# Convolution taps and index scores read from PSUM, group B's gate tiles projected for all tokens at once, and a new order of steps

## The chip, the core and the metric

The kernel runs on one core of one Trainium2 chip. The metric is the device time of one execution in microseconds (us), as the median of several runs. A profile of one execution gives what each engine did and when: TensorE (PE, with its weight loads as PEld), VectorE (DVE), ScalarE (ACT), GpSimd (POOL) and SyncE (SP), which issues the loads.

## What is computed

One layer: an adaptive norm of x (1024 tokens, 1024 channels), one input projection into 3792 columns, two groups of heads, one output projection.

```python
h = rmsnorm(x, g_pre[layer]) * (1.0 + scale[:, None, :]) + shift[:, None, :]
proj = h @ w_in[layer]
(qkv_a, z_a, b_a, a_a, q_b, ckv, z_b, iq, ik, iw) = jnp.split(proj, list(SPLIT_OFFSETS), axis=-1)
o_a = gated_deltanet(qkv_a, z_a, b_a, a_a, ...)     # group A
o_b = dsa_sparse_attention(q_b, ckv, iq, ik, iw, ..., z_b)   # group B
mix = jnp.concatenate([o_a, o_b], axis=-1) @ w_out[layer]

def causal_conv(u, w):          # 4 taps, on q, k and v of group A
    up = jnp.pad(u, ((0, 0), (CONV_W - 1, 0), (0, 0)))
    out = up[:, 0:L] * w[0]
    for j in range(1, CONV_W):
        out = out + up[:, j:j + L] * w[j]
    return out

# the index scores of group B, whose 256 largest choose a query's keys (8 heads of 64)
rel = jnp.einsum('bqhd,bsd->bqhs', iqb, ik)
score = jnp.einsum('bqh,bqhs->bqs', iwb, jax.nn.relu(rel))
```

Group A is a gated DeltaNet over chunks of tokens. Group B attends over the chosen keys, and its output is multiplied by silu(z_b), the gate.

## The kernel before, in words

Channels lie on the partitions and tokens along the rows. A projection (`proj`, L427) takes 128 columns of the weights and one half of the tokens (512) and lays 24 matmuls into one PSUM bank: for each of eight slices of the input a high by high, a high by low and a low by high part of the numbers (L435 to L437), where weights and input are split in two parts that are exact for TensorE. The weights come from memory as `wraw`, and are split into `whi` (a copy, L177 or L179) and `wlo` (a difference, L184).

PSUM has eight banks, under three tags: "pp" with two (projections), "r" with four (scores, recurrence, attention) and "g" with two (transposes and small things). A matmul that begins a new product in a bank waits until the last reader of the product before it in that bank is done.

The program is cut into parts, and each part into steps. The list `PLAN` is an order of steps written by hand: K, Q, V (the projections and convolutions of keys, queries and values for a pair of heads 0 or 1), J (inverses on POOL), M (their merging on PE), R (the recurrence), N and A (norm and gate of group A), I (index queries and scores), S0 and S1 (the searches of each query's 256th largest score, S0 with its sums on ACT for the three longest blocks, S1 with counts on DVE), HQ (queries of group B), HZ (its gates), C (latent keys and values), T (attention), O (output). A step yields to those before it in the list, and a scheduler lays the instructions of the engines out from it. The table `ENGINES` names the engine for single sites ("V" DVE, "A" ACT, "G" POOL). What is on one engine runs in the order laid out, so a row that waits holds up those behind it.

`conv_half` (L730) takes a product of a tile of channels and half of the tokens. It copies the product to a tile `u` in SBUF (that has three columns ahead, for the taps that reach back), writes `cv` = last tap times product, and adds the other three taps from `u`: on DVE one instruction each (`add_scaled`, L193), or on ACT a multiplication into `tmp` (L198) and an addition on POOL (L201). SiLU follows in place (L742). `to_nat` (L789) then turns values by 128 columns, and evicts them as `vn`.

The score of a block of queries is summed head by head: two matmuls (the key's two parts, L585 and L586) into a bank of tag "r", the ReLU into a tile `relu` in SBUF (L589 on ACT, L591 on DVE), and `score += iw * relu` on DVE (L193), or on ACT and POOL. The queries' two parts, `qe` and `qo`, are finished on DVE (L570, L571).

`gate_b` is laid out twice, for the later half of the tokens (HZ0) and for the earlier (HZ1). Each takes the same four tiles of weights, so these are loaded and split twice.

Of the kernel before, what the change touches and what calls it, by code (L numbers as in the profile page):

```python
# [46 lines left out]
for _p in range(2):
    PARTS.update({f"K{_p}": (5, (1, 2)), f"J{_p}": (16, ()), f"Q{_p}": (2, (0, 1)), f"M{_p}": (2, ()), f"V{_p}": (2, (0, 1)),
                  f"R{_p}": (8, ()), f"N{_p}": (2, ()), f"A{_p}": (2, (0, 1)), f"HQ{_p}": (4, (0, 1, 2, 3)),
                  f"HZ{_p}": (4, (0, 1, 2, 3))})  # L50
# [1310 lines left out]
```

## Time and profile before

| | |
|---|---|
| median of three runs | 804.77 us (802.54 to 808.46) |
| profiled execution, span | 872.6 us |
| busy PE | 817.9 us, 94% |
| busy DVE | 634.9 us, 73% |
| busy ACT | 428.0 us, 49% |
| busy POOL | 352.8 us, 40% |
| DMA, all engines' mean | 61 GB/s, 53.32 MB |

The profiled execution is longer than the timed ones: 804.77 / 872.6 = 0.922. The page of the profile gives busy time by engine; views of the trace give groups of instructions, waits, stretches of time and single instructions. A matmul's end is modelled, so that a busy PE may also be a waiting one. An idle stretch of an engine is put down to what released it.

### The profile page before, as it was taken

To read this page: it belongs to the slowest core of one execution; us is meant where nothing else is said; L and a number is where in the kernel's file an instruction comes from. 1 tells how busy PE (TensorE), PEld (TensorE's weight loads), DVE (VectorE), ACT (ScalarE), POOL (GpSimd) and SP (SyncE) were. 2 spreads that over 40 slices of the span, in tenths; PEclk is the share of its full clock that TensorE was granted. 3 is DMA by queue.
4 is the path that set the end of the run, shared out by engine and by line. 5 is a ranking of instruction groups with operands and counts; after the bars stand their busy time and mean duration, and the time that the engine had idled before them with its cause. 6 is when DMAs were issued, how large, how long until landed. Compare 5 with 4: busy or idle time off the path is not lost. (4 is left out here: it accounts for less than half of the span.)

```text
span 872.6 us, 11224 instructions
## 1 busy us (share of the span) xinstructions
PE 817.9 (94%) x3837; PEld 628.7 (72%) x3837; DVE 634.9 (73%) x1548; ACT 428.0 (49%) x840; POOL 352.8 (40%) x350
## 2 busy tenths in 40 slices
PE   2999999989999899998996999999999999999997
PEld 1777787867777667865764768776677898876764
DVE  4987656797673898999979957579866788772112
ACT  5345664442543888567455668551335655631100
POOL 2474352697543733867743111046410302641210
PEclk9776677776776677777676777777777777777777
DMA  9940000100210011101522110001220003213111
GB/s 273 343 136 1 25 25 7 42 1 25 48 49 26 12 39 32 43 1 50 192 72 57 41 49 25 25 25 48 73 73 0 25 10 113 97 54 134 55 49 48
DMA packets 66727, 53.32 MB, mean 61 GB/s; under 512 B 12919, under 2 KB 59117, under 8 KB 66670
## 3 DMA queue, kind: packets, MB, share of 16 engines
q1 hardware_dynamic: 66670, 52.61, 20.0%
q8 instruction: 30, 0.49, 0.2%
q14 instruction: 27, 0.22, 0.1%
HBM read 47.35 MB, written 5.25 MB: 60 GB/s over the span
## 5 line engine op out<-in xcount | busy, mean ns | idle before, releaser
L435 PE MATMUL ps<-h,whi 128*128 128x512 f32 (+2 forms) x448 | 206.3, 462 | 0.7 <-DVE cv L181 0.5
L436 PE MATMUL ps<-h,whi 128*128 128x512 f32 (+2 forms) x448 | 206.8, 462 | 0.0
L437 PE MATMUL ps<-h,wlo 128*128 128x512 f32 (+2 forms) x448 | 204.8, 457 | 0.0
L624 ACT ACTIVATE junk<-score,pat,sgn 128x1024 bf16<-128x1024 f32 (+2 forms) x93 | 105.2, 1131 | 50.3 <-DVE pat L653 43.7
L435 PEld LDWEIGHTS ps<-h,whi 128*128 128x128 f32 (+1 forms) x448 | 91.5, 204 | 35.8 <-issue 1.4
L437 PEld LDWEIGHTS ps<-h,wlo 128*128 128x128 f32 (+1 forms) x448 | 93.8, 209 | 32.1 <-issue 0.7
L436 PEld LDWEIGHTS ps<-h,whi 128*128 128x128 f32 (+1 forms) x448 | 90.9, 203 | 31.9 <-issue 1.2
L184 POOL TENSOR_TENSOR wlo<-wraw,whi 128x1024 fp32r<-128x1024 f32 x20 | 49.0, 2448 | 104.7 <-ACT whi L177 59.8
L201 POOL TENSOR_TENSOR cv<-cv,tmp 128x512 f32<-128x512 f32 x31 | 41.2, 1332 | 64.3 <-ACT tmp L198 23.0
L1273 PE MATMUL ps<-wol,mh 128*128 128x512 f32 x128 | 59.3, 463 | 0.0
L1274 PE MATMUL ps<-woh,ml 128*128 128x512 f32 x128 | 58.1, 456 | 0.0
L1272 PE MATMUL ps<-woh,mh 128*128 128x512 f32 x128 | 57.5, 456 | 0.0
L193 DVE SCALAR_TENSOR_TENSOR score<-relu,iw,score 128x512 f32<-128x512 f32 (+3 forms) x51 | 44.4, 897 | 4.8 <-POOL score L201 3.4
L1276 ACT ACTIVATE junk<-ps 128x512 bf16<-128x512 f32 x16 | 9.5, 596 | 75.9 <-PE ps L1274 70.5
L589 ACT ACTIVATE relu<-ps 128x512 f32<-128x512 f32 (+3 forms) x50 | 25.2, 527 | 42.0 <-PE ps L586 32.3
L877 POOL TENSOR_TENSOR ns<-ns,rk 64x30 f32<-64x30 f32 (+14 forms) x60 | 40.2, 669 | 3.8
L875 POOL TENSOR_TENSOR rk<-ns 64x30 f32<-64x30 f32 (+14 forms) x60 | 39.3, 655 | 3.8
L193 DVE SCALAR_TENSOR_TENSOR cv<-u,cols,cv 128x512 f32<-128x512 f32 x41 | 36.4, 893 | 5.3 <-ACT cv L177 2.2
L177 ACT ACTIVATE pT<-ps 128x512 fp32r<-128x512 f32 (+1 forms) x32 | 17.3, 549 | 38.6 <-PE ps L1228 38.3
L612 DVE TENSOR_SCALAR_CACHE_REDUCE junk<-mask,low 128x640 bf16<-128x640 uint16 (+2 forms) x48 | 35.3, 736 | 0.7
L612 DVE TENSOR_SCALAR_CACHE_REDUCE junk<-mask,pat 128x640 bf16<-128x640 bf16 (+2 forms) x45 | 33.3, 739 | 0.5
L1274 PEld LDWEIGHTS ps<-woh,ml 128*128 128x128 f32 x128 | 25.8, 202 | 9.9
(369 smaller groups left out, 1926.6 us busy)
## 6 DMA issues: line engine op xcount, KB each, us to landing
wraw<-in_w_in_dram SPq DMA_DIRECT2D x37, 512.0 KB, 3.7
wa<-in_w_ada_dram SPq DMA_DIRECT2D x24, 512.0 KB, 7.3
x<-in_x_dram SPq DMA_DIRECT2D x8, 512.0 KB, 4.9
woraw<-in_w_out_dram SPq DMA_DIRECT2D x8, 512.0 KB, 3.4
xr<-in_x_dram SPq DMA_DIRECT2D x8, 512.0 KB, 3.3
out_dram<-y SPq DMA_DIRECT2D x16, 256.0 KB, 2.0
scr<-X SPq DMA_DIRECT2D x16, 32.0 KB, 1.6
ns<-scr SPq DMA_DIRECT2D x2, 256.0 KB, 3.5
```

The costliest lines, as they stand in the source:

```text
L184: (V if engine(site, usual, "GV") == "V" else G).tensor_sub(dst, a, b)
L193: V.scalar_tensor_tensor(o, a, scale, o, op0=ALU.mult, op1=ALU.add)
L201: G.tensor_tensor(o, o, tmp, op=ALU.add)
L435: mm(o, lhsT=hi[:, k, :], rhs=h[:, 0, c0:c1], start=(k == 0), stop=False)
L436: mm(o, lhsT=hi[:, k, :], rhs=h[:, 1, c0:c1], start=False, stop=False)
L437: mm(o, lhsT=lo[:, k, :], rhs=h[:, 0, c0:c1], start=False, stop=(k == NK - 1))
L612: V.tensor_scalar(junk[:, 0:src.shape[1]], src, t, None, op0=ALU.is_ge, op1=ALU.add, accum_out=o)
L624: A.activation(junk[:, 0:(b + 1) * P], score[b], AF.Sign, scale=sg, bias=t, accum_out=o)
L877: G.tensor_tensor(ns[:, 0:i, i + 1:32], ns[:, 0:i, i + 1:32], tmp, op=ALU.add)
L1272: mm(ps, lhsT=mh[:, k, :], rhs=woh[k][:, sl], start=(k == 0), stop=False)
L1273: mm(ps, lhsT=mh[:, k, :], rhs=wol[k][:, sl], start=False, stop=False)
L1274: mm(ps, lhsT=ml[:, k, :], rhs=woh[k][:, sl], start=False, stop=(k == NK - 1))
```

## The change

What the diff does:

- `conv_half` has no `u`. The taps read the product in its PSUM bank, each with 509 to 511 columns, and what reaches back over the border between the halves is taken from a little tile `last` (the first half's last three columns), by three small instructions of 1, 2 and 3 columns. The first tap, the product times the last weight, is as before.
- The ReLU of the scores is written back to its bank, and the sums read it from there; there is no tile `relu`. Where ACT multiplies, it writes to the small tile `tmp`.
- `gate_b` is one part, HZ, of four steps; each takes a tile of weights once and projects both halves of the tokens from it (48 matmuls in a step, in place of 24 in each of eight).
- `PLAN` and `ENGINES` have new entries. Among them `mod02`, by which four additions for the adaptive norm go from DVE to eight small matmuls on PE, and four squares (`sq`) that go from POOL to ACT.

```diff
-PLAN = ("X D0 F X X D1 F F E F K0 K0 K0 K0 K0 I Q0 I J0 J0 J0 J0 Q0 I I J0 I J0 J0 J0 J0 J0 I J0 I J0 J0 I J0 "
+PLAN = ("X D0 F X X F D1 F E F K0 K0 K0 K0 K0 I J0 J0 Q0 I J0 J0 I I J0 J0 J0 I J0 Q0 I J0 I J0 J0 J0 J0 J0 J0 "
...
-    def add_scaled(site, o, a, scale, tmp=None):
-        """o += scale * a"""
-        e = engine(site, "V", "VAG")
-        if e == "V":
+    def add_scaled(site, o, a, scale):
+        if engine(site, "V", "VA") == "V":
             V.scalar_tensor_tensor(o, a, scale, o, op0=ALU.mult, op1=ALU.add)
             return
-        if tmp is None:
-            tmp = sm((P, 512), name="tmp", tag="tmp2k", bufs=2)
-        if e == "A":
-            A.mul(tmp, a, scale)
-        else:
-            G.tensor_scalar(tmp, a, scale, None, op0=ALU.mult)
+        tmp = sm((P, 512), name="tmp", tag="tmp2k", bufs=2)[:, 0:a.shape[1]]
+        A.mul(tmp, a, scale)
         G.tensor_tensor(o, o, tmp, op=ALU.add)
...
-                    rl = blk((P, 2, 512), name="relu")
                     for h, q in ((2 * j, qe), (2 * j + 1, qo)):
                         ps = bank("r", 4)
...
-                        r = rl[:, h % 2]
+                        r = ps
...
-                            add_scaled(f"s{h}{b}{ch}", sc[:, cl], r[:, 0:w], iw[:, b, h:h + 1], r[:, 0:w])
-                    rel(rl)
+                            add_scaled(f"s{h}{b}{ch}", sc[:, cl], r[:, 0:w], iw[:, b, h:h + 1])
...
-    def conv_half(m, u, o, hf, ps, b=None):
+    def conv_half(m, o, last, hf, ps, b=None):
         c0 = hf * 512
         oh = o[:, c0:c0 + 512]
         if b is None:
-            copy(f"u{m}{hf}", u[:, 3 + c0:515 + c0], ps)
             copy(f"o{m}{hf}", oh, ps, convc[:, 3, m:m + 1])
         else:
-            A.activation(u[:, 3 + c0:515 + c0], ps, AF.Identity, bias=b[0])
             A.activation(oh, ps, AF.Identity, scale=convc[:, 3, m:m + 1], bias=b[1])
+        if not hf:
+            if b is None:
+                copy(f"u{m}", last, ps[:, 509:512])
+            else:
+                A.activation(last, ps[:, 509:512], AF.Identity, bias=b[0])
         for j in (2, 1, 0):
-            uj, cj = u[:, c0 + j:c0 + j + 512], convc[:, j, m:m + 1]
-            add_scaled(f"cv{m}{hf}{j}", oh, uj, cj)
+            add_scaled(f"cv{m}{hf}{j}", oh[:, 3 - j:512], ps[:, 0:509 + j], convc[:, j, m:m + 1])
+        if hf:
+            for j in (2, 1, 0):
+                V.scalar_tensor_tensor(oh[:, 0:3 - j], last[:, j:3], convc[:, j, m:m + 1], oh[:, 0:3 - j], op0=ALU.mult,
+                                       op1=ALU.add)
+        elif b is not None:
+            V.scalar_tensor_tensor(oh[:, 0:3], unseen[:, :, m], b[2], oh[:, 0:3], op0=ALU.mult, op1=ALU.add)
         A.activation(oh, oh, AF.Silu)
...
-    def gate_b(hf):
-        for q2 in range(2):
-            zb[2 * hf + q2] = blk((P, 4, 256), name="zb")
+    def gate_b():
+        for q4 in range(4):
+            zb[q4] = blk((P, 4, 256), name="zb")
         for h in range(4):
-            ps = proj(nextw(), hf * 512, (hf + 1) * 512)
-            for q2 in range(2):
-                A.activation(zb[2 * hf + q2][:, h, :], ps[:, 256 * q2:256 * q2 + 256], AF.Silu)
-            served(hf)
+            w = nextw()
+            for hf in (1, 0):
+                ps = proj(w, hf * 512, (hf + 1) * 512)
+                for q2 in range(2):
+                    A.activation(zb[2 * hf + q2][:, h, :], ps[:, 256 * q2:256 * q2 + 256], AF.Silu)
+                served(hf)
```

How this moves instructions is seen at three places.

**The scores on PE.** In the program of before, PE comes from the scores of the first two heads (`qe_1054`, `qo_1055`) to those of the next two (`qe_1373`, `qo_1374`) with nothing between them:

```order
L585 MATMUL ps_1346<-khi_529,qe_1054 128x512
L586 MATMUL ps_1346<-klo_530,qe_1054 128x512
L585 MATMUL ps_1351<-khi_529,qo_1055 128x512
L586 MATMUL ps_1351<-klo_530,qo_1055 128x512
L585 MATMUL ps_1357<-khi_529,qe_1054 128x384
L586 MATMUL ps_1357<-klo_530,qe_1054 128x384
L585 MATMUL ps_1362<-khi_529,qo_1055 128x384
L586 MATMUL ps_1362<-klo_530,qo_1055 128x384
L585 MATMUL ps_1438<-khi_529,qe_1373 128x512
L586 MATMUL ps_1438<-klo_530,qe_1373 128x512
```

In the changed program, the same place on PE (the first heads' `qe_1072`, `qo_1073`, the next ones' `qe_1323`; `ps_1607` and `ps_1668` are projections):

```order
L583 MATMUL ps_1307<-khi_539,qe_1072 128x384
L584 MATMUL ps_1307<-klo_540,qe_1072 128x384
L583 MATMUL ps_1312<-khi_539,qo_1073 128x384
L584 MATMUL ps_1312<-klo_540,qo_1073 128x384
L435 MATMUL ps_1607<-h_499,whi_1317 128x256
L436 MATMUL ps_1607<-h_499,wlo_1318 128x256
L434 MATMUL ps_1668<-h_492,whi_1570 128x512
L583 MATMUL ps_1395<-khi_539,qe_1323 128x512
L584 MATMUL ps_1395<-klo_540,qe_1323 128x512
L435 MATMUL ps_1668<-h_492,whi_1570 128x512
```

Projections now stand between the scores here. The longest run of scores with no projection in it was 9 heads (18 matmuls) at this place, and is now 19 heads (38 matmuls) further on, in the second half of the next two heads and the beginning of those after them.

**The last convolution of values on ACT.** In the program of before, the second half of the tile `cv_3895` (the last tile of values, in V1), between sums of the search S0 (`junk`, `cnt`):

```order
L177 ACTIVATE cv_3895<-ps_3937,cols 128x512
L198 ACTIVATE tmp_3964<-u_3893,cols 128x512
L742 ACTIVATE cv_3895<-cv_3895 128x512
L198 ACTIVATE tmp_3967<-u_3893,cols 128x512
L624 ACTIVATE junk_3665,cnt_2314<-score_1043,pat_2316,sgn_2320 128x1024
L198 ACTIVATE tmp_3970<-u_3893,cols 128x512
L624 ACTIVATE junk_3667,cnt_2314<-score_1044,pat_2316,sgn_2320 128x896
L624 ACTIVATE junk_3669,cnt_2314<-score_1045,pat_2316,sgn_2320 128x768
L742 ACTIVATE cv_3895<-cv_3895 128x512
```

In the changed program the same tile is `cv_3933`:

```order
L174 ACTIVATE cv_3933<-ps_3976,cols 128x512
L192 ACTIVATE tmp_4002<-ps_3976,cols 128x511
L749 ACTIVATE cv_3933<-cv_3933 128x512
L192 ACTIVATE tmp_4005<-ps_3976,cols 128x510
L192 ACTIVATE tmp_4008<-ps_3976,cols 128x509
L621 ACTIVATE junk_3661,cnt_2313<-score_1061,pat_2315,sgn_2319 128x1024
L749 ACTIVATE cv_3933<-cv_3933 128x512
L621 ACTIVATE junk_3663,cnt_2313<-score_1062,pat_2315,sgn_2319 128x896
```

The third tap and the second SiLU now stand ahead of two of the search's sums, and the first row no longer has a copy `u` of DVE beside it.

**The latent keys on PE.** In the program of before, the second group of turns of `cT` (the latents), then gates of HZ1 (`ps_5188`, `ps_5221`, `ps_5379`), and among them the turns of the normed latents `cn`:

```order
L435 MATMUL ps_5188<-h_521,whi_5147 128x512
L436 MATMUL ps_5188<-h_521,whi_5147 128x512
L789 MATMUL ps_5306<-ident,cT_4463 128x128 x4
L437 MATMUL ps_5188<-h_521,wlo_5148 128x512
...
L435 MATMUL ps_5379<-h_521,whi_5215 128x512
L436 MATMUL ps_5379<-h_521,whi_5215 128x512
L789 MATMUL ps_5324<-ident,cn_5298 128x128 x4
L789 MATMUL ps_5331<-ident,cn_5298 128x128 x4
```

In the changed program (gates of HZ: `ps_5339`, `ps_5366`, `ps_5399`, `ps_5426`):

```order
L794 MATMUL ps_5266<-ident,cT_4486 128x128 x4
L434 MATMUL ps_5339<-h_531,whi_5199 128x512
...
L434 MATMUL ps_5366<-h_492,whi_5199 128x512
...
L434 MATMUL ps_5399<-h_531,whi_5333 128x512
...
L434 MATMUL ps_5426<-h_493,whi_5333 128x512
L794 MATMUL ps_5284<-ident,cn_5258 128x128 x4
L794 MATMUL ps_5291<-ident,cn_5258 128x128 x4
```

Between the last turn of `cT` and the first of `cn` there were 48 matmuls of projections (22 of one gate, 24 of the next, 2 of a third), and there are 76 now (three gates of 24 and 4).

## Rows read from the trace of the kernel before

**Rows 1.** The page: the span, and busy time by engine.

```profile
span 872.6 us, 11224 instructions
PE 817.9 (94%) x3837; PEld 628.7 (72%) x3837; DVE 634.9 (73%) x1548; ACT 428.0 (49%) x840; POOL 352.8 (40%) x350
```

**Rows 2.** Stretches: from:to, length, busy us by engine, granted clock, DMA share, GB/s.

```profile
140.00:200.00 60.00, 54.88 (x268) 46.10 (x267) 51.04 (x117) 26.30 (x48) 41.89 (x49) 0.72 0.11 27
200.00:286.00 86.00, 86.00 (x504) 65.15 (x503) 52.26 (x79) 35.76 (x71) 45.10 (x48) 0.72 0.12 32
340.00:440.00 100.00, 93.14 (x392) 70.38 (x391) 99.19 (x272) 62.54 (x133) 71.28 (x81) 0.72 0.23 68
```

**Rows 3.** Waits of PE: line, what released it, total us, times, longest.

```profile
PE ps L934 <- ACT vn L177: 5.2, 1, 5.2
PE ps L585 <- DVE qe L570: 5.1, 2, 3.7
PE ps L789 <- DVE cn L1113: 3.7, 1, 3.7
...
PE ps L934 <- DVE qsb L935: 2.0, 1, 2.0
...
PE ps L1026 <- DVE vn L1023: 1.7, 1, 1.7
```

**Rows 4.** DVE in order of time about 191 us: start, us, instruction, count.

```profile
191.17 5.20 DVE L193 SCALAR_TENSOR_TENSOR score<-relu,iw,score 128x320 f32<-128x320 f32 x3
196.40 0.69 DVE L570 TENSOR_TENSOR qe<-ps,qe 64x512 fp32r<-64x512 f32 x1
```

**Rows 5.** Groups of DVE by form: count | busy us, mean ns | idle before.

```profile
L193 DVE SCALAR_TENSOR_TENSOR cv<-u,cols,cv 128x512 f32<-128x512 f32 x41 | 36.4, 893 | 5.3 <-ACT cv L177 2.2 <-ACT cv L738 1.5 <-POOL cv L201 1.2
...
L193 DVE SCALAR_TENSOR_TENSOR score<-relu,iw,score 128x512 f32<-128x512 f32 x15 | 14.3, 973 | 0.3
...
L193 DVE SCALAR_TENSOR_TENSOR score<-relu,iw,score 128x384 f32<-128x384 f32 x15 | 13.4, 908 | 0.4
...
L653 DVE SCALAR_TENSOR_TENSOR pat<-ok,thr 128x3 int32<-128x3 int32 x31 | 11.9, 383 | 0.1
...
L193 DVE SCALAR_TENSOR_TENSOR score<-relu,iw,score 128x320 f32<-128x320 f32 x11 | 9.7, 902 | 0.7 <-ACT relu L589 0.6
...
L181 DVE TENSOR_SCALAR cv<-ps,cols 128x512 f32<-128x512 f32 x13 | 9.5, 741 | 5.4 <-ACT u L177 5.4
...
L179 DVE COPY u<-ps 128x512 f32<-128x512 f32 x8 | 5.5, 685 | 0.0
...
L851 DVE SCALAR_TENSOR_TENSOR gv<-gv,beta 128x4 f32<-128x4 f32 x8 | 1.3, 164 | 0.1
```

**Rows 6.** DVE, two kinds: count, shortest/median/longest ns, first and last start.

```profile
L193 DVE SCALAR_TENSOR_TENSOR cv<-u,cols,cv x41: 733/749/1644, 75.1 to 451.0; 128x512 f32<-128x512 f32 x41
...
L181 DVE TENSOR_SCALAR cv<-ps,cols x13: 728/744/752, 111.0 to 583.4; 128x512 f32<-128x512 f32 x13
```

**Rows 7.** Stretches behind two waits of PE, and one without, columns as in rows 2.

```profile
471.00:480.00 9.00, 6.68 (x44) 5.48 (x45) 8.71 (x27) 5.22 (x12) 2.37 (x1) 0.52 0.20 56
...
600.00:608.00 8.00, 8.00 (x30) 5.56 (x29) 7.93 (x8) 1.61 (x3) 3.67 (x3) 0.75 0.23 66
...
198.00:206.00 8.00, 8.00 (x23) 6.03 (x23) 5.95 (x9) 0.60 (x1) 7.37 (x10) 0.60 0.04 13
```

**Rows 8.** ACT and DVE in order of time, 455 to 471 us, columns as in rows 4.

```profile
455.82 0.69 ACT L177 ACTIVATE cv<-ps,cols 128x512 f32<-128x512 f32 x1 [0.93 <-DVE u L179]
...
461.39 0.71 ACT L198 ACTIVATE tmp<-u,cols 128x512 f32<-128x512 f32 x1
...
470.92 0.35 ACT L177 ACTIVATE vn<-ps,gv 128x128 f32<-128x128 f32 x1
...
455.11 0.68 DVE L179 COPY u<-ps 128x512 f32<-128x512 f32 x1
...
466.48 0.27 DVE L928 MEMSET T<- 32x256 f32 x1
```

More of the change, by code (lines that the diff above doesn't have):

```diff
@@ L48 @@
     PARTS.update({f"K{_p}": (5, (1, 2)), f"J{_p}": (16, ()), f"Q{_p}": (2, (0, 1)), f"M{_p}": (2, ()), f"V{_p}": (2, (0, 1)),
[L49 to L50 removed]
+                  f"R{_p}": (8, ()), f"N{_p}": (2, ()), f"A{_p}": (2, (0, 1)), f"HQ{_p}": (4, (0, 1, 2, 3))})
 PARTS["K0"], PARTS["Q0"] = (5, ()), (2, ())
@@ L53 @@
     PARTS.update({f"T{_p}": (4, ()), f"O{_p}": (2, ())})
-ENGINES = {"ad10": "V", "ad11": "V", "ad20": "V", "ad30": "V", "ad40": "V", "ad51": "V", "cT0": "V", "cT1":
[42 rows of a table removed]
+ENGINES = {"ad10": "V", "ad11": "V", "ad20": "V", "ad21": "V", "ad30": "V", "ad51": "V", "cT0": "V", "cT1": "V",
[41 rows of a table added]
 SITES = {}
@@ L221, in rsqrt @@
         G.tensor_tensor(o, o, mhalf[:, 0:n], op=ALU.pow)
-    offs = {"I": OFF_IQ, "C": OFF_CKV}
+    offs = {"I": OFF_IQ, "C": OFF_CKV, "HZ": OFF_ZB}
     for a in range(2):
-        offs.update({f"HQ{a}": OFF_QB, f"HZ{a}": OFF_ZB})
+        offs.update({f"HQ{a}": OFF_QB})
         for n, off in (("K", OFF_K), ("Q", OFF_Q), ("V", OFF_V), ("A", OFF_ZA)):
@@ L235, in hybrid_kernel @@
             for g in range(2):
-                readers[g] += not n.endswith(f"{1 - g}") or n[0] != "H"
+                readers[g] += n != f"HQ{1 - g}"
         done[n] += 1
@@ L288, in hybrid_kernel @@
     convc = cols[:, 32:80].rearrange("p (j m) -> p j m", j=4)
+    unseen = const.tile([P, 3, 12], F32, name="unseen")
+    taps = const.tile([P, 12], F32, name="taps")
+    V.tensor_copy(unseen[:, 2], convc[:, 0])
+    V.tensor_tensor(unseen[:, 1], convc[:, 0], convc[:, 1], op=ALU.add)
+    V.tensor_tensor(unseen[:, 0], unseen[:, 1], convc[:, 2], op=ALU.add)
+    V.tensor_tensor(taps, unseen[:, 0], convc[:, 3], op=ALU.add)
     gkv_c = cols[:, 80:81]
@@ L592, in index @@
                         if h == 0:
-                            copy(f"s0{b}{ch}", sc[:, cl], r[:, 0:w], iw[:, b, 0:1], "V", "VAG")
+                            copy(f"s0{b}{ch}", sc[:, cl], r[:, 0:w], iw[:, b, 0:1], "V", "VA")
                         else:
-                            add_scaled(f"s{h}{b}{ch}", sc[:, cl], r[:, 0:w], iw[:, b, h:h + 1], r[:, 0:w])
-                    rel(rl)
+                            add_scaled(f"s{h}{b}{ch}", sc[:, cl], r[:, 0:w], iw[:, b, h:h + 1])
                 if b == 6:
@@ L766, in first_halves @@
                 mm(pb0[:, 0:1], lhsT=raw0[h][:, k, :], rhs=shc[:, k:k + 1], start=(k == 0), stop=(k == NK - 1))
-            b0 = sm((P, 2), name="b0")
+            b0 = sm((P, 3), name="b0")
             V.tensor_copy(b0[:, 0:1], pb0[:, 0:1])
-            V.tensor_tensor(b0[:, 1:2], b0[:, 0:1], convc[:, 3, m:m + 1], op=ALU.mult)
+            V.tensor_tensor(b0[:, 1:2], pb0[:, 0:1], taps[:, m:m + 1], op=ALU.mult)
+            V.tensor_scalar(b0[:, 2:3], pb0[:, 0:1], -1.0, None, op0=ALU.mult)
             first.append(conv_new())
-            conv_half(m, *first[h], 0, ps0[h], (b0[:, 0:1], b0[:, 1:2]))
+            conv_half(m, *first[h], 0, ps0[h], (b0[:, 0:1], b0[:, 1:2], b0[:, 2:3]))
             if h > 1:
@@ L778, in conv_rest @@
         m = EARLY[h][1]
-        u, o = first[h]
-        conv_half(m, u, o, 1, proj(w0[h], 512, 1024))
+        o, last = first[h]
+        conv_half(m, o, last, 1, proj(w0[h], 512, 1024))
         served(1)
-        rel(u, *w0[h])
+        rel(*w0[h])
         return o
@@ L1314, in hybrid_kernel @@
     mixA, late = {}, {}
-    gens = {"I": index(), "S0": fewer(search((7, 6, 5), True), 2), "S1": fewer(search((4, 3, 2), False), 2),
+    gens = {"HZ": gate_b(), "I": index(), "S0": fewer(search((7, 6, 5), True), 2), "S1": fewer(search((4, 3, 2), False), 2),
             "G": residual_gate(), "C": latents(), "W": load_wout(),
@@ L1319, in hybrid_kernel @@
         gens.update({f"K{a}": keys(a), f"J{a}": fewer(invert(a), 2), f"Q{a}": queries(a), f"M{a}": merge(a), f"V{a}": values(a),
-                     f"R{a}": recur(a), f"N{a}": norm(a), f"A{a}": gate_a(a), f"HQ{a}": queries_b(a), f"HZ{a}": gate_b(a)})
+                     f"R{a}": recur(a), f"N{a}": norm(a), f"A{a}": gate_a(a), f"HQ{a}": queries_b(a)})
     for b in range(NT):
```

13 lines of the change are left out of this document (5 added, 8 removed), and 92 rows, old and new, of tables (ENGINES, PLAN).

## The prediction, made before the changed kernel ran

> **What bounds the kernel now.** I read the engines' busy time first [rows 1]: PE is busy for 817.9 of 872.6 us, so the change, which leaves PE nearly all its matmuls (eight small ones come on top), can win only what PE loses to waits and to a lower clock. Then the table of stretches [rows 2]: from 200 to 286 us PE is busy all the time while DVE has 52 of 86, so an instruction less on DVE is worth nothing there. From 340 to 440 it is the other way round, DVE 99.19 of 100 and PE 93.14, and from 140 to 200 DVE has 51.04 of 60 and PE loses 5.1. Then the waits of PE [rows 3]: the reader is to see that the longest, beside those of the start, are 5.2 us before the merge M1 (for the last turned values, `vn`), 5.1 us in the scores (for `qe`), 3.7 us for the latents `cn`, 2.0 us in the merge itself, and 1.7 us in a norm. Together they make 17.7 us. Last the clock behind such a wait [rows 7]: 0.75 in a stretch without a wait, 0.60 for 8 us behind the wait for `qe`, 0.52 for 9 us behind the merge's. At 0.75 the first would have done its work in 8 x 0.60 / 0.75 = 6.4 us, the second in 6.2 us, so 1.6 and 2.8 us are the waits' echo. PE's bill of the places that DVE holds up is therefore 17.7 + 1.6 + 2.8 = 22.1 us.
>
> **What the change does to DVE's work.** 41 taps on DVE now read PSUM. No row of before adds a scaled PSUM tile to an SBUF tile with a column as the scale. The nearest is the first tap, PSUM times a column, at 741 ns; below it is the plain copy out of PSUM, 685 ns; above is no change, 893 ns, which is what the taps from SBUF took on the mean [rows 5]. I take 741: 41 x 0.152 = 6.2 us less (0 to 8.5). That a PSUM operand should make it shorter is seen in the spread [rows 6]: taps from SBUF ran from 733 to 1644 ns, the ones from PSUM from 728 to 752, so what goes is the tail, not the body. The sums of scores are 15 x 973, 15 x 908 and 11 x 902 ns [rows 5]; at 741 at most each, 3.5 + 2.5 + 1.8 = 7.8 us less (0 if they keep their time). Eight copies `u` on DVE at 685 ns go: 5.5 us. Against that stand 36 additions of 1 to 3 columns for the border. The nearest row is four columns at 164 ns, the farthest three columns at 383 ns [rows 5]: 5.9 to 13.8 us; I take 5.9, because the 383 ns are of integers behind sums for the search. Four additions of the start leave DVE for PE, two ReLUs and two sums of scores come to it, the splits of weights and small preparations about cancel. DVE's sum is -6.2 - 7.8 - 5.5 + 5.9 = -13.6 us, with the ends -16 (all at the cheap ends) and +8 (only the copies gone, and dear borders: -5.5 + 13.8).
>
> Why the tail goes is put in the Trainium skill, "SBUF — State Buffer", section "SBUF: two separate sides": DVE and GpSimd share a pair of ports by an exclusive lock, which a DVE instruction with two SBUF inputs needs against a GpSimd one that reads SBUF. The spread of rows 6 agrees. But the same skill, "VectorE: DVE Perf Modes", section "Rules for kernel authors", advises against the change: it lets one copy a matmul's output to SBUF first if many operations follow, and its errata table has an estimate of (120 - 58) cycles at 0.96 GHz, 65 ns, more for each read of PSUM. By that the tap would be 749 + 65 = 814 ns, and 41 of them would win 3.2 us in place of 6.2. The first tap's 741 ns, read from PSUM, speaks for the row.
>
> **What it is worth, place by place.** *Start:* eight matmuls of one column in place of four additions; nothing either way, since the loads of the first stretch set it (1 us each way).
>
> *Scores.* The wait for `qe` comes of three sums of scores that took 5.20 us in a row, with `qe` queued behind them [rows 4]. On PE no projection stands there to cover it. In the changed order projections do, and the next heads' `qe` is finished on DVE some 60 rows ahead of the first sum that needs it. So 5.1 + 1.6 = 6.7 us go. But the bank of a head is now held through its ReLU and its sum. In the run of 19 heads further on, DVE has to do 13 sums, 6 ReLUs, a tap and a small row before the last head's bank is free: 13 x 0.741 + 6 x 0.685 + 0.741 + 0.164 = 14.6 us. PE comes to that head after 18 pairs of matmuls at no more than 2 x 0.27 us (8 us for 30 [rows 7]), 9.7 us. It waits for the other 4.9 us, and with the echo of 1.6 us that is 6.5. Taken as zero in the sum, between -6.7 (DVE comes to the run early) and +6.
>
> *The stretch 340 to 440.* DVE is full there and arrives up to 13.6 us earlier at its end; the 1.7 us for the norm's `vn` go: -1.7. The taps of this stretch themselves win little.
>
> *Before M1.* The second half of V1's last tile is late for three reasons, one behind the other [rows 8]: ACT's first row on it (455.82) waited 0.93 us for DVE's copy `u` (455.11), the third tap (461.39) stood behind a sum of the search, and the values were evicted until 471.3, from the turns of which M1's bank came free. In the changed order there is no copy to wait for, and the third tap and the SiLU stand ahead of the search's sums. What is late next is M1's own tile `T` on DVE, ready at 466.48 + 0.27 = 466.75, where PE's wait began at 471.32 - 5.15 = 466.17. So at least 0.6 us of the 5.2 stay unless DVE is early. All of it with the wait inside the merge and the echo is 5.2 + 2.0 + 2.8 = 10.0. I take 7.0: the inner wait of 2.0 is for a copy on a full DVE, which nothing here takes away, and 1.0 is left for `T`. The bounds are 0 and 10.
>
> *Latents.* PE has 76 matmuls of projections between the turns of `cT` and of `cn`, where it had 48: 28 x 0.27 = 7.6 us of cover more for a wait of 3.7 [rows 3]. -3.7; 0 if DVE, which keeps the same squares, sums and scale for `cn`, is as much later.
>
> *Gates.* Four loads and splits of weights go (two copies on ACT and two on DVE, the differences mostly on POOL). PE waits for none of them [rows 3], so nothing; it is hidden under projections, and PE's 24 matmuls for a half remain. The loads are one buffer ahead, as before.
>
> Sum: -1.7 - 7.0 - 3.7 = -12.4 us of 872.6, so 860.2. The median of the timed runs stands to the profiled span as 804.77 / 872.6 = 0.922, and this gives 793 us.
>
> **The rivals.**
> *A, the forecast*: 793 us; its own range is 785 to 799.
> *B, the work goes where PE does not wait for it.* DVE's rows are taken off in stretches where PE is full, and before M1 the search's counts, which fill DVE from 340 to 440, take the room, so that `T` and `vn` are as late as before. Only the latents' wait goes: 872.6 - 3.7 = 868.9, which is 801 us. For it: DVE's 99.19 of 100 are mostly not taps. Against it: ACT's first row on the tile no longer waits for DVE.
> *C, slower: the four banks of the scores become the bound.* A bank is turned round in a pair of matmuls, a ReLU and a sum: 0.54 + 0.685 + 0.741 = 1.97 us, and four banks allow 4 x 0.54 = 2.16. Only 0.19 us are left. If every sum stands behind two other rows of DVE of 0.741, it is 3.45 / 4 = 0.86 us a head, 0.32 more than PE needs, and for 80 heads 26 us. Then DVE is what is late, M1's wait stays, and only the latents win: 872.6 + 26 - 3.7 = 894.9, which is 825 us. It decides against the change from about a row and a half of DVE ahead of each sum. For it: DVE at 85% from 140 to 200 [rows 2], and 19 heads in a run. Against it: projections between most other heads, whose 0.27 us each give PE something else to do. The Trainium skill, "TensorE: Matmul & The Clock Gate", section "A second HAM failure mode: psum-queue depth-cycling", has such a case: short idle times between groups of matmuls that cycle through banks make the clock go up and down, and the throughput falls. The clock of 0.60 and 0.52 behind waits [rows 7] agrees with it.
> *D, all of the bill goes*: the new run of scores costs nothing since DVE is early, and the merge runs through: 872.6 - 22.1 = 850.5, which is 784 us; with DVE's ends a little below, to 776.
>
> **The numbers.** A 0.46, B 0.26, C 0.14, D 0.14. About 1% is what a measurement of this kernel can tell from no change, that is 797 and 813 us. A lies below 797 for nine tenths (0.42), D wholly: faster 0.56. B and the rest of A: 0.30. C: 0.14. The range goes from D's far end, 776, to 811, which leaves out C's price and a little of D.
>
> **What would show it.** Taps and sums from PSUM near 0.74 us at 512 columns, without a tail; no wait for `qe` at the first change of heads, and a wait of some us in the run of 19 heads; the wait ahead of the merge M1 down from 5.2 to about 1 us; no wait for `cn`. The forecast is wrong if the borders' small rows take more than 0.38 us each, if PE's waits in the scores add up to more than about 10 us, or if the clock sinks in more places than it did.

## The result: faster by 4.2%, three times what was forecast

| | us | ratio to before, 95% interval |
|---|---|---|
| before (median of 4 runs, 802.54 to 809.58) | 806.62 | |
| changed (median of 4 runs, 766.95 to 775.65) | 771.25 | 0.9582 [0.9521, 0.9642] |
| forecast | 793 (776 to 811) | |

The time lies below the range, and 35 us were won where 12 (in the profile's time) were forecast. The kernel before was profiled once more among the experiments (called "before, again" below), and this profile is needed to read the one of the changed kernel: the first one had a granted clock of 0.737 and a span of 872.6 us, this one 0.927 and 803.9 us, and the four runs of the changed kernel 0.927 to 0.946.

### The profile page after: what moved, and what is told of

Its sections match the earlier page's. It is cut to its first block, busy times and chain, and to the rows that moved or that the text cites. A ratio compares the mean times of both kernels' runs of the same rounds, so it can differ in the third digit from the quotient of the medians.

```text
span 768.9 us, 11288 instructions
## 1 busy us (share of the span) xinstructions
PE 690.2 (90%) x3853; PEld 575.8 (75%) x3853; DVE 592.3 (77%) x1567; ACT 416.1 (54%) x838; POOL 313.6 (41%) x342
## 3 DMA queue, kind: packets, MB, share of 16 engines
q1 hardware_dynamic: 62510, 50.51, 21.8%
## 4 chain that ended last, share of the span: by engine, by line
PE 50%; DVE 30%; ACT 4%; POOL 4%; issue 4%; DMA 2%; SPq 0%; DVEq 0%; POOLq 0%; ACTq 0%
PE ps L434 7%; DVE junk L609 7%; PE ps L435 7%; PE ps L436 7%; PE ps L1279 4%; PE ps L1280 4%; PE ps L1281 4%; DVE cv L189 2%; PE ps L583 1%; PE ps L1235 1%; ACT junk L621 1%; PE ps L584 1%; DVE score L189 1%; DVE cv L745 1%; DMA woraw<-in_w_out_dram 1%
## 5 line engine op out<-in xcount | busy, mean ns | idle before, releaser
L434 PE MATMUL ps<-h,whi 128*128 128x512 f32 (+2 forms) x448 | 183.0, 409 | 15.0 <-DVE cv L745 7.5
L435 PE MATMUL ps<-h,whi 128*128 128x512 f32 (+2 forms) x448 | 180.9, 404 | 0.5 <-POOL h L181 0.5
L436 PE MATMUL ps<-h,wlo 128*128 128x512 f32 (+2 forms) x448 | 179.5, 401 | 0.4 <-DVE wlo L181 0.4
L435 PEld LDWEIGHTS ps<-h,whi 128*128 128x128 f32 (+1 forms) x448 | 88.7, 198 | 17.7 <-POOL h L181 1.0
L181 POOL TENSOR_TENSOR wlo<-wraw,whi 128x1024 fp32r<-128x1024 f32 (+1 forms) x16 | 39.3, 2455 | 93.0 <-ACT whi L174 34.2
L193 POOL TENSOR_TENSOR cv<-cv,tmp 128x510 f32<-128x510 f32 (+2 forms) x31 | 36.7, 1185 | 62.3 <-ACT tmp L192 44.1
L1280 PE MATMUL ps<-wol,mh 128*128 128x512 f32 x128 | 50.2, 392 | 0.0
L189 DVE SCALAR_TENSOR_TENSOR score<-ps,iw,score 128x384 f32<-128x384 f32 (+3 forms) x53 | 33.6, 649 | 13.4 <-POOL score L193 8.4
L587 ACT ACTIVATE ps<-ps 128x384 f32<-128x384 f32 (+3 forms) x48 | 23.7, 509 | 36.1 <-PE ps L584 35.7
L189 DVE SCALAR_TENSOR_TENSOR cv<-ps,cols,cv 128x511 f32<-128x511 f32 (+2 forms) x41 | 30.1, 739 | 3.6 <-POOL cv L193 1.4
L1223 ACT ACTIVATE pr<-pr,st 128x896 f32<-128x896 f32 (+7 forms) x32 | 24.7, 773 | 12.3 <-DVE st L1222 12.1
L1279 PEld LDWEIGHTS ps<-woh,mh 128*128 128x128 f32 x128 | 24.0, 188 | 6.2 <-ACT mh L174 1.5
```

What stands on the lines that cost most here:

```text
L181: (V if engine(site, usual, "GV") == "V" else G).tensor_sub(dst, a, b)
L193: G.tensor_tensor(o, o, tmp, op=ALU.add)
L434: mm(o, lhsT=hi[:, k, :], rhs=h[:, 0, c0:c1], start=(k == 0), stop=False)
L435: mm(o, lhsT=hi[:, k, :], rhs=h[:, 1, c0:c1], start=False, stop=False)
L436: mm(o, lhsT=lo[:, k, :], rhs=h[:, 0, c0:c1], start=False, stop=(k == NK - 1))
L1279: mm(ps, lhsT=mh[:, k, :], rhs=woh[k][:, sl], start=(k == 0), stop=False)
```

## The profile after, beside that of before taken again

The page of the changed kernel, and then that of the kernel before, again:

```profile
span 768.9 us, 11288 instructions
PE 690.2 (90%) x3853; PEld 575.8 (75%) x3853; DVE 592.3 (77%) x1567; ACT 416.1 (54%) x838; POOL 313.6 (41%) x342
```

```profile
PE 709.5 (88%) x3837; PEld 587.6 (73%) x3837; DVE 635.8 (79%) x1548; ACT 424.4 (53%) x840; POOL 353.9 (44%) x350
```

PE is idle for 803.9 - 709.5 = 94.4 us before, not for 54.7 as in [rows 1], and for 78.7 after: 15.7 of the 35 us are idle time. The other 19.3 are busy time for the same matmuls. By the mean granted clocks 709.5 x (1 - 0.927 / 0.945) = 13.5 of them are the clock; this is an estimate.

Stretches of before, again: from:to, length, busy us of PE, PEld, DVE, ACT, POOL, granted clock, DMA share, GB/s. The borders are the first product of a score, the first of the merge M0, the first of M1, and the first turn of `cn`:

```profile
0.00:139.00 139.00, 114.39 (x542) 93.55 (x542) 101.09 (x198) 72.25 (x105) 63.91 (x61) 0.90 0.41 126
139.00:230.80 91.80, 81.55 (x437) 68.97 (x436) 81.90 (x149) 44.43 (x86) 73.28 (x83) 0.98 0.15 35
230.80:449.00 218.20, 187.71 (x1012) 150.12 (x1012) 195.57 (x540) 135.60 (x276) 119.97 (x126) 0.89 0.19 53
449.00:581.80 132.80, 116.17 (x725) 95.22 (x725) 106.91 (x267) 77.90 (x174) 34.53 (x20) 0.91 0.13 38
581.80:803.90 222.10, 209.67 (x1126) 179.74 (x1126) 150.31 (x397) 94.26 (x202) 62.24 (x61) 0.97 0.22 72
```

The same stretches of the changed kernel:

```profile
0.00:128.40 128.40, 104.53 (x543) 85.46 (x544) 94.77 (x199) 67.78 (x102) 59.65 (x61) 0.95 0.45 136
128.40:218.60 90.20, 84.06 (x443) 70.64 (x442) 75.28 (x170) 38.23 (x73) 51.69 (x75) 0.96 0.15 36
218.60:431.70 213.10, 183.69 (x1020) 149.34 (x1020) 189.16 (x559) 138.15 (x286) 108.19 (x127) 0.89 0.18 53
431.70:568.60 136.90, 126.00 (x774) 103.79 (x774) 105.22 (x259) 83.20 (x183) 34.53 (x20) 0.95 0.13 35
568.60:768.90 200.30, 191.95 (x1076) 166.61 (x1076) 127.87 (x384) 88.75 (x196) 59.56 (x60) 1.00 0.22 72
```

The differences are -10.6, -1.6, -5.1, +4.1 and -21.8 us, -35.0 in all. Fifty matmuls have moved from the last stretch to the one ahead of it, so these two count together: -17.7, of which 9.8 are idle time (29.1 to 19.3). The start, for which the forecast had nothing, gives 10.6, and what lies behind M1 the half of all. The scores and the stretch to M1, where most of the forecast lay, give 6.7.

Waits of PE in the changed kernel (line, releaser, us in total, times, longest); [rows 3] answers to them:

```profile
PE ps L434 <- DVE cv L745: 7.5, 2, 6.0
...
PE ps L434 <- ACT za L1042: 4.7, 1, 4.7
PE ps L346 <- DVE acc L338: 4.5, 4, 2.5
PE ps L939 <- DVE qsb L940: 4.4, 1, 4.4
...
PE ps L434 <- DVE cv L189: 2.2, 1, 2.2
...
PE ps L794 <- DVE cn L1118: 0.8, 1, 0.8
...
PE ps L939 <- ACT vn L174: 0.3, 1, 0.3
```

and in the kernel before, again:

```profile
PE ps L435 <- ACT cv L177: 6.6, 5, 2.6
PE ps L789 <- ACT cv L742: 5.8, 4, 2.7
PE ps L347 <- DVE acc L339: 5.8, 2, 5.4
PE ps L934 <- ACT vn L177: 5.7, 1, 5.7
PE ps L1235 <- DVE pT L179: 5.2, 2, 3.3
...
PE ps L435 <- DVE whi L179: 5.0, 1, 5.0
PE ps L585 <- DVE qe L570: 4.4, 3, 2.7
...
PE ps L789 <- DVE cn L1113: 3.9, 1, 3.9
PE ps L946 <- ACT T L942: 3.7, 1, 3.7
```

The waits for `qe`, `whi` and `cn`, for `vn` ahead of M1 and for `pT` in the attention are gone or nearly so, and the one for `acc` at the start is shorter. The two largest of before belong to the convolutions. The turns behind a SiLU waited for it (`cv`, L742, 5.8 us), and no longer do. Projections waited for a bank that `cv` still had to read (L177, 6.6 us); this has grown to 9.7 us (L745 and L189), since the taps now read that bank too, and the wait for the gate `za`, which frees such a bank, is 4.7 us (1.3 before). In the first profile the waits for `cv`, `pT` and `T` are 1.6 us or less each, and the one for a gate's `whi` does not stand there.

DVE's groups by form in the changed kernel (count, busy us, mean ns, idle before), for [rows 5], and the spread of the taps and of the border's rows (shortest/median/longest ns):

```profile
L189 DVE SCALAR_TENSOR_TENSOR score<-ps,iw,score 128x512 f32<-128x512 f32 x15 | 11.1, 747 | 1.8 <-ACT ps L587 1.5
...
L189 DVE SCALAR_TENSOR_TENSOR cv<-ps,cols,cv 128x511 f32<-128x511 f32 x15 | 11.1, 743 | 2.0 <-ACT last L740 1.3 <-ACT last L174 0.7
...
L745 DVE SCALAR_TENSOR_TENSOR cv<-last,cols,cv 128x2 f32<-128x2 f32 x12 | 6.0, 498 | 0.0
...
L650 DVE SCALAR_TENSOR_TENSOR pat<-ok,thr 128x3 int32<-128x3 int32 x31 | 5.3, 173 | 0.3
...
L745 DVE SCALAR_TENSOR_TENSOR cv<-last,cols,cv 128x1 f32<-128x1 f32 x12 | 5.3, 442 | 0.0
...
L745 DVE SCALAR_TENSOR_TENSOR cv<-last,cols,cv 128x3 f32<-128x3 f32 x12 | 3.2, 267 | 0.0
```

```profile
L189 DVE SCALAR_TENSOR_TENSOR cv<-ps,cols,cv x41: 648/742/751, 70.3 to 414.4; 128x511 f32<-128x511 f32 x15, 128x509 f32<-128x509 f32 x15, 128x510 f32<-128x510 f32 x11
L745 DVE SCALAR_TENSOR_TENSOR cv<-last,cols,cv x36: 190/212/1675, 96.2 to 426.4; 128x1 f32<-128x1 f32 x12, 128x2 f32<-128x2 f32 x12, 128x3 f32<-128x3 f32 x12
```

## What the experiments showed

**1. The kernel before, again.** No edit.

> The kernel before, once more, with a profile. Theory 'clock': the profiled execution of before, with a granted clock of 0.737, was not like the timed ones. Then this one has a clock above 0.9, a span near 805 us, PE busy for some 700 to 740 us in place of 818, and the waits of PE for DVE, ACT and POOL in the middle add up to 60 us or more in place of about 25. Rival 'typical': the clock is again near 0.74 and the span near 870 us, and the gain of 35 us has to be found in the waits that the first profile showed.

805.64 us, clock 0.927, span 803.9, PE busy for 709.5. "Clock" holds: the profile that the forecast rests on was not like the timed runs. What that hides is seen at the split of a gate's weights. PE and then DVE of this profile, in order of time (start, us, instruction):

```profile
571.31 0.39 PE L437 MATMUL ps<-h,wlo 128*128 128x512 f32 x1
576.70 0.77 PE L435 MATMUL ps<-h,whi 128*128 128x512 f32 x1 [5.00 <-DVE whi L179]
```

```profile
570.02 3.02 DVE L722 SCALAR_TENSOR_TENSOR score<-score,pat,eq 128x1024 f32<-128x1024 f32 x1
...
575.87 0.68 DVE L179 CAST whi<-wraw 128x1024 fp32r<-128x1024 f32 x1
```

The split stands behind the search's last rows on DVE. At this clock PE gets through a projection's matmuls at 0.23 us each, where it took 0.27 in [rows 7], and is there 5 us ahead of the split. At the lower clock it came after it. DVE is busy for as long in both profiles (634.9 and 635.8 us), so PE, which is through sooner, waits longer for it: the idle time is 94.4 us for 54.7. Not every single wait grows: the one for `qe` is 4.4 us for 5.1.

**2. The pieces, in the order of before and in the new one.** Seven kernels, each the program of before or the changed one with pieces put in or taken back: taps in PSUM (`conv_half`), scores in PSUM, gates in one set, order (list of steps and table of engines). The edits are the parts of the diff above.

> All three changes of code (taps from PSUM, scores from PSUM, one set of gate steps), but the order of steps and the engines of before; the gates' four steps stand where those of the later half stood. Theory 'code': most of the 35 us come from work taken off DVE, so this has at least two thirds of them: 770 to 783 us. Rival 'order': the new list of steps and engines makes the gain, and this stays at 795 us or above.

> The new order of steps, the new engines and the one set of gate steps, but taps from the copy in SBUF and scores from the ReLU tile in SBUF as before. Theory 'code': 793 to 805 us. Rival 'order': 770 to 785 us.

> The kernel before with the taps read from PSUM and nothing else. Theory 'code' at the timed clock: DVE's copies and the taps' tail go (11.7 us), the border's small rows come (5.9 us by the forecast, 14 us by the profile of the changed kernel), and chains get shorter by the copy; 790 to 800 us. If the bank held longer costs more than this wins: 805 us or above.

> The changed kernel with the taps read from the copy u in SBUF again; scores from PSUM, gates in one set, new order stay. Theory 'the taps carry it': without them the order of steps is laid for a cheaper convolution than there is, and this stands at 795 us or above. Rival 'the scores carry it': 771 to 782 us.

> The changed kernel with the ReLU's tile in SBUF again and the sums of scores read from it; taps from PSUM, gates in one set, new order stay. Theory 'the taps carry it': 771 to 785 us, since the sums of scores lie where PE has projections. Rival 'the scores carry it': 790 us or above.

> The kernel before with the gates of group B in one set of four steps, and nothing else; the four steps stand where the later half's stood. By the second profile of before, PE waits 5.0 us for a split of weights (whi) and 3.9 us for cn among the gates and latents. Theory 'gates': both go, with what the clock gives back: 792 to 798 us. Rival (my prediction's zero): 802 us or above.

> The kernel before with the scores summed from PSUM and nothing else. By rival C of the prediction the four banks become the bound: 812 us or above. By the cheaper sums (about 8 to 13 us off DVE): 795 to 803 us. If the order of before is laid for the old code and any change in it disturbs more than it wins: 806 to 815 us.

| taps | scores | gates | order | us | ratio, interval | label |
|---|---|---|---|---|---|---|
| | | x | old | 796.6 | 0.9898 [0.9866, 0.9931] | b_hz |
| | x | | old | 806.4 | 1.0009 [0.9984, 1.0034] | b_score |
| x | | | old | 819.7 | 1.0179 [1.0129, 1.0228] | b_conv |
| x | x | x | old | 811.4 | 1.0084 [1.0061, 1.0107] | a_oldorder |
| | | x | new | 805.1 | 1.0005 [0.9979, 1.0031] | a_neworder_only |
| | x | x | new | 783.8 | 0.9730 [0.9679, 0.9781] | a_noconv |
| x | | x | new | 790.0 | 0.9804 [0.9755, 0.9852] | a_noscore |
| x | x | x | new | 771.3 | 0.9582 [0.9521, 0.9642] | the change |

Neither "code" nor "order" is right: all the code in the old order is slightly slower than before (0.8%), and the new order with the gates alone gives nothing. In the new order the scores win 19 to 21 us (790.0 to 771.3, 805.1 to 783.8) and the taps 13 to 15 (783.8 to 771.3, 805.1 to 790.0), nearly the same with and without each other. In the old order the scores win nothing, the taps lose 14, and the gates alone win 8 to 10 (by the ratio and by the medians); in their profile the wait for a gate's `whi` is gone and the one for `cn` is 0.9 us. How much of this is the pieces and how much a list that was made for one set of pieces is not told apart here: each list came with its own code, and none was written anew for a part of it.

**3. List or engines.** The changed code with only the one or the other of before.

> The changed code and the new table of engines, with the list of steps of before (the gates' four steps where the later half's stood). The new list and the new engines together are worth 40 us on the changed code (811.4 to 771.3). Theory 'steps': the list makes it, and this stands at 800 us or above. Rival 'engines': 775 to 785 us.

> The changed code and the new list of steps, with the table of engines of before. Theory 'steps': 771 to 782 us. Rival 'engines': 800 us or above. Between the two (about 790): both are needed.

811.3 us (1.0067 [1.0041, 1.0092]) with the old list, 793.8 us (0.9845 [0.9799, 0.9891]) with the old engines. On the changed code the list is worth 40 us with the new engines and 18 with the old ones, the engines 22 once the list is new, and nothing without it (a_oldorder's 811.4).

**4. The wait for za.** With the taps in PSUM and the old list, one wait of PE is 12 to 13.5 us long. PE, and ACT ahead of it, in b_conv:

```profile
436.91 0.80 PE L437 MATMUL ps<-h,whi 128*128 128x512 f32 x1 [13.51 <-ACT za L1047]
```

```profile
427.45 1.24 ACT L626 ACTIVATE junk<-score,pat,sgn 128x1024 bf16<-128x1024 f32 x1 [5.40 <-DVE pat L655]
...
436.29 1.05 ACT L1047 ACTIVATE za<-ps 128x512 f32<-128x512 f32 x2
```

`za` frees a projection's bank, and stands behind sums of the search S0 that wait for DVE. The edit for a_oldorder:

```diff
- J1 N0 Q1 S1 S0 A0 G S1 A0 J1 G J1
+ J1 N0 Q1 A0 A0 S1 S0 G S1 J1 G J1
```

> The changed code in the order of before, in which PE waited 12.0 us for ACT's za (the gate of group A, which frees the bank of a projection), here with one edit: the two steps A0 stand ahead of the steps of the searches S0 and S1 beside them. Theory 'queue': za came late because it stood behind sums of the search on ACT, which wait for DVE; put ahead of them it frees the bank, and 8 to 15 us of the 811 go: 796 to 803 us. Rival 'bank': the projection would wait as long for a bank that the taps hold; 807 us or above.

819.7 us (1.0159 [1.0105, 1.0213]). The time is the rival's, but its mechanism was not seen either: the wait for `za` fell to 4.4 us, and a longer one came behind it, for the residual gate on DVE:

```profile
456.94 3.47 PE L1064 MATMUL ps<-gac,ones 128*128 128x512 f32 x4 [13.97 <-DVE gac L1059]
```

So `za` is where PE met DVE's lateness, and this edit only moved the place.

**5. Fewer border rows.** Three additions on DVE become one; POOL sums the three columns when `last` is there, in 60 small rows more. The part of the edit on DVE:

```diff
-            for j in (2, 1, 0):
-                V.scalar_tensor_tensor(oh[:, 0:3 - j], last[:, j:3], convc[:, j, m:m + 1], oh[:, 0:3 - j], ...)
+            V.tensor_tensor(oh[:, 0:3], oh[:, 0:3], last[:, 3:6], op=ALU.add)
```

> The changed kernel, with the three border additions of a tile (36 on DVE, 14.5 us busy in its profile, and 6.0 us of PE's waits end with one) replaced by one: POOL sums the three columns ahead, when the first half's last columns are there. If DVE's time is what PE waits for: 24 rows of about 0.4 us less, 762 to 768 us. If the rows of POOL come in the way of DVE or of the inverses: 775 us or above.

794.9 us (0.9865 [0.9812, 0.9919]): 23 us slower than the change, though DVE has 24 rows less. The wait for `za` grew from 4.7 to 15.1 us. What DVE does from M0 to M1 shows where the time went. Stretches as above, a_corr:

```profile
222.20:462.20 240.00, 193.72 (x1021) 157.85 (x1022) 213.57 (x612) 145.13 (x298) 117.08 (x157) 0.82 0.18 49
```

DVE's busy time there is 213.6 us in place of 189.2. Counted row by row in the trace, 373 rows of the search stand in the stretch, and 312 in the changed kernel. That M1 waits for these rows is argued from this and not shown.

**6. DVE's work up to M1.** Over 14 profiles up to here the length of the stretch from M0 to M1 is DVE's busy time in it and 20 to 28 us more: 196 of 218 before, 189 of 213 after, 209 of 233 in b_conv, 180 of 200 in b_score, 207 of 232 in a_oldorder_a0, 214 of 240 in a_corr. What differs most in it are the search's rows (298 before, 312 after, 379 in b_conv, 377 in a_oldorder_a0): S1's counts have a place wherever the scheduler sees DVE free. So the two steps G (9 us of DVE, needed at the end only) were put behind M1 in both kernels, and a small edit tested whether any edit at all upsets the layout.

```diff
- ... A0 G J1 J1 A0 G S0 S1 S1 ... M1 S1 M1 S0 S1 R1 HQ1 S0 ...
+ ... A0 J1 J1 A0 S0 S1 S1 ... M1 S1 M1 S0 G S1 R1 HQ1 G S0 ...
```

> The changed kernel with the two steps G (the residual gate, seven additions of 1.28 us on DVE, needed only by the output) moved from before the merge M1 to behind it. Theory 'DVE full': M1 comes 7 to 10 us earlier, DVE has room behind M1 (105 of 137 us busy), and the time is 760 to 766 us. Rival 'laid anew': the edit costs a layout that was good, 775 us or above.

> The kernel before with the same edit: the two steps G behind M1. Theory 'DVE full': M1, at 449 us in its profile, comes 7 to 10 us earlier, 795 to 800 us. Rival 'laid anew': 810 us or above. No difference (803 to 808): DVE's work before M1 is not what M1 waits for.

> The changed kernel with one eviction of 128 by 256 (about 0.4 us) on ACT in place of DVE, and nothing else. If a layout is stable under a small edit: 769 to 774 us. Theory 'laid anew': 780 us or above, and then a part of each difference between single pieces is the layout's.

> The kernel before with the same small edit. Stable layout: 803 to 808 us. Theory 'laid anew': 812 us or above.

With G late, 803.4 us (0.9984 [0.9950, 1.0018]) and 817.6 us (1.0164 [1.0098, 1.0230]): M1 came no earlier (434.0 us for 431.7, and 447.0 for 449.0), as 46 and 45 rows of the search filled the room (102 us of them for 87 and 91), and the stretch from M1 to `cn`, where G now is, got 12 and 23 us longer. With G late the changed kernel's last stretch is 14 us longer too (214.4 for 200.3), and the cause of that stays open. The small edit changes nothing: 767.9 us (0.9567 [0.9500, 0.9633]) and 806.1 us (1.0014 [0.9982, 1.0045]), so the layouts do not break at any edit whatever; one edit on each does not show more.

**7. The search held back.** Two steps of S1 stand behind M1's first step, and a little copy holds them there: it reads M1's first transpose, and writes to the tile that the next counts write to.

```diff
+            if pr == 1 and h == 0:
+                late["hold"] = sm((P, 1), name="hold")
+                V.tensor_copy(late["hold"], tf[:, 0, 0:1])
...
+                if "hold" in late:
+                    V.tensor_copy(cn_[:, 0:1], late.pop("hold"))
```

> b_conv (the kernel before with the taps from PSUM, 819.7 us), with two steps of the search S1 laid behind M1's first step, and held there by one little copy on DVE that reads M1's first transpose. In the order laid out, 201 rows of the search stand between M0's transposes and M1's first product needed from DVE, where b_conv has 270 and the kernel before 211. Theory 'search ahead of M1': M1 comes some 14 us earlier than in b_conv (470 us), and the time goes to 800 to 808 us. Rival 'the taps hold the bank': the wait for it stays or moves to another place, 815 us or above.

> The changed kernel with the same edit; 201 rows of the search ahead of M1 in place of 224. Theory 'search ahead of M1': M1 comes 5 to 7 us earlier, and as DVE has room behind M1 the time goes to 762 to 767 us, if the search S0 does not get later by it (its last masks are written at 567 us, where the first attention begins). If the search's end is what counts next: 771 us or above.

b_conv_hold: 812.2 us (1.0075 [1.0039, 1.0111]), a_hold: 776.1 us (0.9666 [0.9598, 0.9733]). b_conv and then b_conv_hold, from M0 to M1:

```profile
237.10:470.20 233.10, 190.04 (x992) 153.50 (x991) 209.00 (x614) 139.19 (x285) 103.89 (x124) 0.82 0.17 49
```

```profile
237.60:456.10 218.50, 186.24 (x993) 150.47 (x992) 181.91 (x506) 141.02 (x288) 104.80 (x124) 0.83 0.18 51
```

M1 comes 14 us earlier than in b_conv, as expected, and of this 7.5 us reach the end, since what was held back has to be done behind M1 (134 us to `cn` in place of 129). That is the half of what the taps alone lose in the old order. DVE has 36.6 us free in the stretch now, and PE's idle time there is 32.3 us, where b_conv has 43.1 and before has 30.5, so the rest has another cause, which stays open: `za` is still waited for (7.1 us). The scores' stretch is 12 us longer than before in both (103.5 in b_conv, for 91.8), but 34 matmuls more stand in it, and its idle time is 13.2 for 10.2 us. In the changed kernel M1 comes 1.6 us earlier and nothing is won: with 276 rows of the search in the stretch, DVE's busy time fell by 7 us and its length by 2. There the search is not what M1 waits for.

No kernel tried is clearly faster than the change; a_kn10's 767.9 us lies within the spread of its runs.

## Why the prediction was wrong, by its steps

**The last step failed, and with it the first.** "The median of the timed runs stands to the profiled span as 804.77 / 872.6 = 0.922, and this gives 793": a ratio of 0.922 is not a scale to multiply by, it says that the profiled execution ran at another clock (0.737 for 0.927). All waits, and so the whole bill of 22.1 us, were read from the wrong one. In the second profile PE is idle for 94.4 us, not 54.7, and waits that the first has at 2 us or less, or not at all, stand there for `cv` (6.6 and 5.8 us), `acc` (5.8), `pT` (5.2), `whi` (5.0) and `T` (3.7). What the change would win at the lower clock, for which the sum was made, no run shows.

**"Start: nothing either way"** was wrong by the most: -10.6 us. Its reason, the loads, holds for the first 50 us, in which the DMA engines' mean share is 0.98; from there to 62 us it is 0.23. In the first profile the wait for `acc` is a small one (1.7 us); at the timed clock it is 5.4 us, and 2.5 after the four additions left DVE (2.6 in a_neworder_only, 5.4 in b_conv). This is 3 us of the 10.6. In this pair of profiles the start's idle time falls by 0.7 us only (24.6 to 23.9), and the rest is busy time at a higher clock, 0.95 for 0.90. Behind the wait for `acc` the clock of before is at its lower level, 0.50 (1.2 GHz), for 8 us, and after the change it is not for as long; before, then after:

```profile
62.00:70.00 8.00, 7.94 (x29) 6.62 (x30) 6.32 (x12) 6.04 (x9) 5.96 (x5) 0.50 0.12 36
```

```profile
59.80:70.00 10.20, 10.13 (x43) 8.04 (x44) 8.63 (x14) 6.67 (x9) 6.97 (x6) 0.63 0.10 28
```

From 90 to 100 us it is 0.66 before and 1.00 after. That the shorter wait is what keeps the clock up is likely and not shown: b_hz, b_score and b_glate, with the start of before, are idle there for 29.4 to 29.6 us at 0.91 to 0.92. The first score comes 4.3 us earlier by the order with the gates and 5.4 by the taps alone (139.0 to 134.7 and 133.6), the latter with 15 matmuls fewer ahead of it.

**"Gates: PE waits for none of them, so nothing"** was wrong: alone they win 8 to 10 us, by the wait for `whi` that the first profile does not show, and by `cn`.

**The order had no term of its own.** The forecast took it in at the waits it moves. It is what the code needs: with the gates in one set, taps and scores together cost 15 us in the old order (796.6 to 811.4) and win 34 in the new one (805.1 to 771.3). Why the list has this effect is shown in part only (experiments 4 to 7).

**DVE's sum was near for the rows that it counts, and the whole was three times as large.** Taps took 743 ns for the 741 forecast, sums of 512 columns 747 at 741; the border's rows were at the dear end, 14.5 us for 5.9 taken and 13.8 as the bound. Taps -6.9, sums of scores -12.9, copies -5.5 and borders +14.5 make -10.8; DVE's busy time fell by 43.5. A row of the kind that the prediction missed ("No row of before adds a scaled PSUM tile to an SBUF tile") does stand in the first profile: `ctl` (L1124), a PSUM tile times a column less an SBUF tile, takes 743 ns for 512 columns.

Rows that the change does not touch got shorter, as the search's `pat` from 357 ns in the second profile of before to 173. The traces show why, row by row. A row of DVE with two operands in SBUF that starts while POOL is at work mostly lasts until POOL's row has ended. The 18 border rows of the changed kernel with no row of POOL beside them take 207 to 220 ns. All twelve that take over 400 ns end 13 to 22 ns after a row of POOL; over all kernels 123 of 124 border rows above 300 ns end within 23 ns of one. Not every row of POOL does this: the four border rows that start in the middle of a `gv` row of POOL (L869) take 190 to 214 ns. Of the 41 taps from PSUM 15 have such a row beside them, and none takes over 751 ns. Counted as what each row takes above the median of its kind with no POOL beside it, these waits make 87 us of DVE's time in the second profile of before and 51 in the changed kernel, which is an estimate. POOL's rows got shorter as well: the 120 of the inverses, which the change leaves alone, take 64.2 us for 80.3, so the waiting seems to go both ways. The 383 ns of [rows 5], which I put down to integers, are a mean of such rows, 19 without POOL beside them at 155 ns and 12 with it at 745.

PE's wait of 6.0 us that ends with a border row is not that row's work. PE, POOL and DVE in the changed kernel, in order of time:

```profile
361.61 0.76 PE L434 MATMUL ps<-h,whi 128*128 128x512 f32 x1 [6.02 <-DVE cv L745]
```

```profile
356.37 1.26 POOL L193 TENSOR_TENSOR cv<-cv,tmp 128x511 f32<-128x511 f32 x1 [2.25 <-ACT tmp L192]
```

```profile
356.83 0.82 DVE L745 SCALAR_TENSOR_TENSOR cv<-last,cols,cv 128x2 f32<-128x2 f32 x1
...
359.86 0.87 DVE L609 TENSOR_SCALAR_CACHE_REDUCE junk<-mask,pat 128x640 bf16<-128x640 bf16 x1
...
360.73 0.74 DVE L189 SCALAR_TENSOR_TENSOR cv<-ps,cols,cv 128x509 f32<-128x509 f32 x1
361.38 0.21 DVE L745 SCALAR_TENSOR_TENSOR cv<-last,cols,cv 128x3 f32<-128x3 f32 x1
```

The border row at the end takes 0.21 us. The tap ahead of it, which reads the projection's bank, stands behind rows of the search on DVE, and the border row of two columns ahead of those (356.83, 0.82 us) ends 0.02 us after POOL's addition.

Of the two pages cited there, the rows bear out the first: the Trainium skill's "SBUF — State Buffer", "SBUF: two separate sides", lets a DVE instruction with two SBUF inputs wait for a GpSimd one that reads SBUF, and the taps from PSUM have no tail (648 to 751 ns) where the ones from SBUF had one [rows 6]; the border's rows, all in SBUF, run from 190 to 1675 ns. The copy to SBUF first, which the Trainium skill's "VectorE: DVE Perf Modes", "Rules for kernel authors", names for many operations on a product, had no gain for a tap here: 743 ns from PSUM is no more than the 749 that was the median from SBUF, and not the 814 worked out from that page.

**Right by place:** no wait for `qe` (4.4 to none, 5.1 in the first profile), waits of 3.8 us in the run of 19 heads where 4.9 were worked out (6.1 in all the scores, 2.9 for sums and 3.2 for `tmp`), M1's wait for `vn` from 5.7 to 0.3, `cn` from 3.9 to 0.8, and none for the norm's `vn` (3.1 before). But the inner wait of the merge, kept at 2.0, grew to 4.4, so that of the 7.0 us taken before M1 only 2.5 came as idle time (7.7 to 5.2).

**The rivals.** B's mechanism was hardly seen: the search's rows did take DVE's room in other kernels, but here 312 stand ahead of M1 for 298, and M1's wait went all the same. C's was seen at 6 us, with a clock of 0.96 for 0.98 in the scores, and 0.945 for 0.927 on the whole, so the fall of the clock from the Trainium skill's "TensorE: Matmul & The Clock Gate", "A second HAM failure mode: psum-queue depth-cycling", that was set beside it is not what decided this case. D, all of the bill, came nearest and was still short by 13 us, since the bill was.

## What to carry to other kernels

Compare the profiled execution's span and granted clock with the timed runs before any wait is read; where they differ by 8%, engines that are busy for as long at either clock are later against PE than the profile shows, and a change that takes work off them can be worth more. Where a scheduler fills gaps, a piece of code and the order have to be measured together: freed time on an engine may be filled with work that nobody waits for yet, ahead of what the next stage needs. A wait that an edit removes is only a cause when the next one does not grow by as much.
